# One product in two column parts near the start of long matmul runs: 64 and 192 columns in place of 256, in 44 places

## The chip, the core and the metric

The kernel runs on one core of a Trainium2 chip. TensorE (PE) multiplies, VectorE (DVE), ScalarE (ACT) and GpSimd (POOL) do the rest, and SyncE (SP) issues most of the transfers. The metric is the device time of one execution in microseconds (us).

## The reference

Two blocks act on x, 256 positions of 1024 features. The first is a layer with three attention branches and a feed-forward part with a short convolution; the second has two layers, each of a gated linear recurrence and a chunked matrix memory. Cut to the products that matter here:

```
x = x + rms_norm(merged(mla(h), dilated(h), memory(h)) @ w_o)      # h = rms_norm(x) ; w_in feeds the branches
x = x + rms_norm(gated_conv(rms_norm(x) @ w_ffn_up) @ w_ffn_down)
for l in range(2):                                                  # the second block
    rg_x, rg_z, ml_x, ml_o, ml_z = split((rms_norm(x) * (1 + scale) + shift) @ w_in_2[l])
    y = concat(rglru(conv(rg_x)) * silu(rg_z), mlstm(ml_x, ml_o) * silu(ml_z))
    x = x + gate * (y @ w_out_2[l])
```

All of it is float32.

## The kernel before

**Products.** Every weight matrix is read from HBM once, in blocks of 128 x 1024 numbers (`load`, lines 249 to 262). SP issues the transfer into a `raw` buffer, ACT rounds it to `hi` (line 257), DVE makes the rest `lo` = raw - hi (line 260). There are four buffers of each. The activations are split in the same way (H and L, or pairs of `s` tiles). A product in full precision is then three products of parts, hi·H, hi·L and lo·H, and `prod` (line 263 on) issues them for four blocks of 128 in the sum at a time: four matmuls of the first kind, four of the second, four of the third, so twelve. Each matmul has its own weights of 128 x 128, which are loaded just before it (the profile's PEld), and sends 256 columns through them (512 in a few places). All of them stand on line 269:

```
for b in range(0, len(terms), 4):
    for x, y in ((0, 2), (0, 3), (1, 2)):
        for t in terms[b:b + 4]:
            pe.matmul(dst, lhsT=t[x], rhs=t[y], start=(first and i == 0), stop=(last and i == n - 1))
            i += 1
```

**Callers.** `proj` makes 256 output features from two calls of `prod`, 24 matmuls each where the sum is over 1024 features: 48 in a row. `proj_long` has the activations as weights and the matrix as the moving side, two blocks of 128 positions, twelve matmuls a call. `proj_first` goes through `prod` too, one term at a time.

**Stages**, with the start in the profiled execution: the memory query `w_memq` (38 us) and then `w_c`; attention and gates (70); `w_o` (about 333); `w_up`, 22 projections of 48 matmuls, f = 0 by `proj_first` (358); `w_down` (503); then for each of two layers the input projections `w_mlx` and `w_rgx` (558 and 773), the small block products and gates, `w_rgz` (four projections, the last at 692 and 907), `w_mlz` (four, with two products of `of_head`, line 979, before each later one), and `w_out` (722 and 936).

**Order.** A scheduler places each engine's instructions from a model of how long each takes, and they then run in that order. Stretches under `urgent()` are placed early. Within a stretch on the TensorE the order is that of the code.

Of the kernel before, what the change touches and what calls it, by code (L numbers as in the profile page):

```python
# [19 lines left out]
S = 256  # L20
D = 1024
KT = D // P
# [4 lines left out]
URGENT = 1000  # L27
RAW, HI, LO = 4, 4, 4
FENCE = 4
STREAM, LOADED = 0, 16  # L30
FILL = dict(xn=8, cst=24, s=16, y=48, sx=16, pt=48, M=16, pts=56)
HOLD = 3
# [8 lines left out]
ADA_OUT = ((1, 3), (1, 3), (1,), ())  # L41
# [69 lines left out]
LONG = (256, 256, 256, 256)  # L111
# [87 lines left out]
def block_kernel(ctx: ExitStack, tc: tile.TileContext, T: dict, out: bass.AP):  # L199
    nc = tc.nc  # L200
    pe, act, dve, pool, dma = nc.tensor, nc.scalar, nc.vector, nc.gpsimd, nc.sync
# [59 lines left out]
        fence["n"] -= 1  # L261
        return hi, lo

    def prod(dst, terms, first=True, last=True):
        n, i = 3 * len(terms), 0
        for b in range(0, len(terms), 4):
            for x, y in ((0, 2), (0, 3), (1, 2)):
                for t in terms[b:b + 4]:
                    pe.matmul(dst, lhsT=t[x], rhs=t[y], start=(first and i == 0), stop=(last and i == n - 1))  # L269
                    i += 1  # L270

    def proj(name, j, kt, H, L, blks=None):
        nb = kt // 4
        if blks is None:
            blks = [load(T[name][j * nb + b]) for b in range(nb)]
        ps = mm_tile()
        for m in range(2):
            prod(ps[:, m], [
                (blks[k // 4][0][:, (k % 4) * 256 + m * P:][:, :P], blks[k // 4][1][:, (k % 4) * 256 + m * P:][:, :P], H(k), L(k))
                for k in range(kt)  # L280
            ])
        return ps

    def urgent(on=True):

        return tc.high_priority(offset=URGENT) if on else nullcontext()

    def proj_long(name, kt, j, H, L, hold=0, beside=(), pieces=LONG, at=16):

        w = pieces[j]  # L290
        ps = [mm_tile().rearrange("p a b -> p (a b)")[:, :w] for _ in range(2)]
        blks = _long_blocks(kt, pieces)[j]
        nb = len(blks)
        held = {}

        def part(b, t):
            tb = slice(t * P, (t + 1) * P)
            hi, lo = held[b]
            prod(ps[t], [(H(k)[:, tb], L(k)[:, tb], hi[:, i * w:(i + 1) * w], lo[:, i * w:(i + 1) * w])
                         for i, k in enumerate(blks[b][1])], b == 0, b == nb - 1)  # L300

        for b, (n, ks) in enumerate(blks):
            held[b] = load(T[name][n][:, :len(ks) * w], at)
            if b in beside:
                ada_steps(1)
            if b < nb - hold:
                for t in range(2):
                    part(b, t)
        for t in range(2):
            for b in range(nb - hold, nb):  # L310
                part(b, t)
        return ps
# [42 lines left out]
    H, L = kth(HT[0]), kth(HT[1])  # L355
# [171 lines left out]
    with tc.tile_pool(name="l1", bufs=1) as l1, tc.tile_pool(name="pS", bufs=1) as pS:  # L527
# [54 lines left out]


        for j in range(2):
            ps = proj("w_memq", j, KT, H, L)
            act.mul(mem_kq[:, 4 + 2 * j:6 + 2 * j], ps, HD_SCALE)


# [5 lines left out]
        for quarter in (0.0, 0.25):  # L594
# [10 lines left out]
            t = l1.tile([P, S], F32, name=f"trig{len(trig)}")  # L605
# [285 lines left out]
    def post_norm(name, kt, Hf, Lf, hold, g, sums, nxt, beside):  # L891
        z = rows_of(6)
        n = len(LONG) - 1
        acc = small.tile([P, 2, n + 1], F32, name="accn", tag="accn", bufs=2)
        for j in range(n + 1):
            jj = slice(LONG_AT[j], LONG_AT[j + 1])
            ps = proj_long(name, kt, j, Hf, Lf, hold, beside[j])
            if j == n:
                pre = [load(T[nxt][b]) for b in range(2)]
            else:  # L900
                for t in range(2):
                    sq = square_sum(ps[t], acc[:, t, j:j + 1])
                    dve.tensor_tensor(out=z[:, t, jj], in0=ps[t], in1=g[:, jj], op=ALU.mult)
            if j == 0:
                root_table(sq)
        x_sum = small.tile([P, 2, 2], F32, name="xsum", tag="xsum", bufs=2)
        stat = [Rstd(acc[:, t]) for t in range(2)]
        fl = Flip()
        for t in range(2):
            with urgent():  # L910
                square_sum(ps[t], acc[:, t, n:n + 1])
                ins = dve.tensor_tensor(out=z[:, t, jj], in0=ps[t], in1=g[:, jj], op=ALU.mult)
                rz = stat[t].get()
                for i, (a, b) in enumerate(PARTS):
                    dve.scalar_tensor_tensor(out=xn[:, t, a:b], in0=z[:, t, a:b], scalar=rz, in1=xn[:, t, a:b], op0=ALU.mult, op1=ALU.add)
                    if sums:
                        square_sum(xn[:, t, a:b], x_sum[:, t, i:i + 1])
                r = Rstd(x_sum[:, t]).get() if sums else None
            fl.add(t, r)
        return x_sum, fl, pre, ins  # L920
# [18 lines left out]
    aL = [slot(i, F32R, LOADED) for i in (3, 4, 5)]  # L939
    with tc.tile_pool(name="fp", bufs=2) as fp:  # L940
        for f in range(FT):
            ps = proj("w_up", f, KT, H, L) if f else proj_first(pre, H, L)
            u, z, w = (fp.tile([P, 2, S], F32, name=n, tag=n) for n in ("fu", "fz", "fw"))
            if f:
                with urgent():
                    dve.tensor_tensor(out=u, in0=ps, in1=rs.unsqueeze(1).to_broadcast([P, 2, S]), op=ALU.mult)  # L946
            else:
                for i in range(2):
                    dve.tensor_tensor(out=u[:, i], in0=ps[i], in1=rs, op=ALU.mult)
            for i in range(2):  # L950
                c = f + FT * i
                act.activation(z[:, i], u[:, i], AF.Identity, scale=col("conv_w", 88 + c), bias=col("conv_b", c))  # L952
                act.activation(w[:, i], u[:, i], AF.Identity, scale=col("conv_w", c))
                dve.scalar_tensor_tensor(out=z[:, i, 1:], in0=u[:, i, :S - 1], scalar=col("conv_w", 44 + c), in1=z[:, i, 1:], op0=ALU.mult, op1=ALU.add)  # L954
            pool.tensor_tensor(out=z[:, :, 2:], in0=z[:, :, 2:], in1=w[:, :, :S - 2], op=ALU.add)  # L955
            t = one()
            act.activation(t, z[:, 0], AF.Silu)
            dve.tensor_tensor(out=t, in0=t, in1=z[:, 1], op=ALU.mult)
            split(aH[f // 8][:, f % 8], aL[f // 8][:, f % 8], t)
# [59 lines left out]
    for l in range(2):  # L1019
# [42 lines left out]
        def mem_input(j):  # L1062
            jj = slice(2 * j, 2 * j + 2)
            if j:
                ps = proj(f"w_mlx{l}", j, KT, H, L)
                with urgent():
                    split(xmH[:, jj], xmL[:, jj], ps)
                ps = [ps[:, 0], ps[:, 1]]
            else:
                ps = proj_first(pre, H, L)  # L1070
                for m in range(2):
                    split(xmH[:, m], xmL[:, m], ps[m])
            cv = two()
            conv4(cv, ps, l, "ml_conv_w_2", "ml_conv_b_2", j)
            t = two()
            act.activation(t, cv, AF.Silu)
            split(xcH[:, jj], xcL[:, jj], t)
# [199 lines left out]
        sq = [numerator(0), numerator(1)]  # L1277
        for j in range(4):
            jj = slice(2 * j, 2 * j + 2)
            ps = proj(f"w_rgz{l}", j, KT, H, L)  # L1280
            silu_into(yrH[:, jj], yrL[:, jj], ps, hs[:, jj])
            if j < 2:
                norm_sums(j, sq[j])
                sq.append(numerator(j + 2))
            elif j == 2:
                norm_sums(2, sq[2])
                norm_sums(3, sq[3])
                with urgent():
                    dve.scalar_tensor_tensor(out=da, in0=ms[:, 0:S], scalar=1.0 / 256.0, in1=da, op0=ALU.mult, op1=ALU.add)
                    r0, w0 = one(), one()  # L1290
                    act.activation(r0, da, AF.Sqrt)
                    dve.reciprocal(r0, r0)
                    dve.tensor_tensor(out=w0, in0=r0, in1=r0, op=ALU.mult)
                    dve.scalar_tensor_tensor(out=w0, in0=w0, scalar=-0.5, in1=da, op0=ALU.mult, op1=ALU.mult)
                    dve.scalar_tensor_tensor(out=da, in0=w0, scalar=1.5, in1=r0, op0=ALU.add, op1=ALU.mult)
                    dp = in_parts("M", da)
            if l == 0:
                ada_steps(ADA_RGZ[j])
        ymH, ymL = slot(2, F32R, LOADED), slot(3, F32R, LOADED)
        for j in range(4):  # L1300
            jj = slice(2 * j, 2 * j + 2)
            ps = proj(f"w_mlz{l}", j, KT, H, L)
            pb = of_head(j, dp)
            for m in range(2):
                dve.scalar_tensor_tensor(out=hn[:, 2 * j + m], in0=hn[:, 2 * j + m], scalar=col("ml_norm_g_2", 8 * l + 2 * j + m),
# [10 lines left out]
        for j in range(n + 1):  # L1316
            jj = slice(LONG_AT[j], LONG_AT[j + 1])
            if j == n:
                ada_steps(50 - n_ada[0])
            ps = proj_long(f"w_out{l}", 2 * KT, j, lambda k: (yrH[:, k] if k < 8 else ymH[:, k - 8]),  # L1320
                           lambda k: (yrL[:, k] if k < 8 else ymL[:, k - 8]), 2 + l, () if l else ADA_OUT[j])
            if j == n:
                if l == 0:
                    pre = [load(T["w_mlx1"][b]) for b in range(2)]
# [43 lines left out]
```

## Time and profile before

| | us |
|---|---|
| median of 3 runs | 984.3 (982.62 to 986.07) |
| the profiled execution's own time | 990.15 |
| span of the profile, first to last instruction | 988.4 |
| PE busy in the span | 957.2 |
| PEld (weight loads) busy | 920.0 |
| DVE busy | 727.8 |
| ACT busy | 628.4 |

The profiled execution took 5.85 us more than the median of the runs that were timed. Busy times of PE are of pipelined instructions that overlap each other: a matmul's record is about 0.28 us long, and the next one starts after some 0.11 us. The distance from start to start, here called the pace, is what counts.

### The profile page before, as it was taken

Reading aid. Unit: us, or ns where it says so; the run is one execution under the profiler, and the core shown is the slowest. Engines: PE = TensorE matmul, PEld = TensorE weight load, DVE = VectorE, ACT = ScalarE, POOL = GpSimd, SP = SyncE. Lnnn points to the kernel's source line nnn. Section 1 sums busy time; section 2 is a strip of 40 time slices with the busy share of each in tenths; the row PEclk is TensorE's granted clock in tenths of the full one; section 3 lists DMA queues with packets and bytes.
Section 4 is the critical chain, followed back from the end, with each engine's and each line's share of the span. In section 5 each row is a group of like instructions: output and inputs, shape, how many; then the busy total and the mean of one; then the engine's idle time right before and its main releaser. Section 6 shows DMA issues by size and latency. Waiting matters only on the chain.

```text
span 988.4 us, 19653 instructions
## 1 busy us (share of the span) xinstructions
PE 957.2 (97%) x7880; PEld 920.0 (93%) x7880; DVE 727.8 (74%) x1283; ACT 628.4 (64%) x1042; POOL 53.1 (5%) x61
## 2 busy tenths in 40 slices
PE   7999999999999999999989999999999999999997
PEld 5999999899989989999989899898999988899997
DVE  5856776568475988878866798688976798687744
ACT  7666555453345578888753786895644776976552
POOL 0000000000000001121200000000001000000031
PEclk9999999999999999999999999999999999999999
DMA  8654566777776755555667365345786365235551
GB/s 298 210 183 141 176 231 194 242 242 227 245 259 192 254 187 189 193 189 179 204 221 244 123 219 174 124 140 190 254 254 215 124 191 170 97 119 193 188 175 63
DMA packets 53371, 190.74 MB, mean 193 GB/s; under 512 B 6080, under 2 KB 6464, under 8 KB 53280
## 3 DMA queue, kind: packets, MB, share of 16 engines
q1 hardware_dynamic: 52272, 185.17, 57.5%
q0 software_dynamic: 1008, 4.33, 1.4%
q8 instruction: 61, 1.00, 0.4%
q14 instruction: 30, 0.25, 0.1%
HBM read 188.42 MB, written 1.05 MB: 192 GB/s over the span
## 4 chain that ended last, share of the span: by engine, by line
PE 74%; DMA 9%; DVE 9%; ACT 4%; issue 3%; POOL 0%; DVEq 0%; SPq 0%; ACTq 0%; POOLq 0%
PE mm L269 64%; DMA raw<-in_w_ada 6%; DVE lo L260 4%; DMA raw<-in_w_down 1%; ACT hi L257 1%; PE sm L1059 1%; DVE raw L506 1%; DMA raw<-in_w_dv 1%; PE sm L1217 1%; DMA raw<-in_w_mlx 1%; PE sm L1268 1%; PE sm L269 1%; DVE two L1016 1%; PE sm L676 1%; PE sm L1259 0%
## 5 line engine op out<-in xcount | busy, mean ns | idle before, releaser
L260 DVE TENSOR_TENSOR lo<-raw,hi 128x1024 fp32r<-128x1024 f32 (+2 forms) x300 | 362.2, 1219 | 105.8 <-ACT hi L257 102.8
L257 ACT CAST hi<-raw 128x1024 fp32r<-128x1024 f32 (+2 forms) x300 | 308.6, 1039 | 159.8 <-PE mm L269 84.4
L269 PE MATMUL mm<-H,hi 128*128 128x256 f32 x1456 | 237.3, 281 | 0.1
L269 PE MATMUL mm<-H,lo 128*128 128x256 f32 x1456 | 233.6, 279 | 1.4 <-DVE lo L260 1.4
L269 PE MATMUL mm<-L,hi 128*128 128x256 f32 x1456 | 234.5, 279 | 0.4 <-DVE L L489 0.2
L269 PEld LDWEIGHTS mm<-H,hi 128*128 128x128 f32 x1456 | 198.3, 189 | 2.2 <-DVE s L1016 0.8
L269 PEld LDWEIGHTS mm<-H,lo 128*128 128x128 f32 x1456 | 197.3, 188 | 1.6 <-DVE lo L260 1.6
L269 PEld LDWEIGHTS mm<-L,hi 128*128 128x128 f32 x1456 | 197.6, 188 | 1.1 <-DVE L L489 0.6
L269 PE MATMUL mm<-hi,s 128*128 128x256 f32 (+1 forms) x1032 | 149.4, 285 | 0.2 <-ACT s L496 0.2
L269 PEld LDWEIGHTS mm<-hi,s 128*128 128x128 f32 x1032 | 132.6, 189 | 2.1 <-ACT s L496 0.4
L506 DVE CUSTOM_DVE_ANT_0 raw<-raw,c_act 128x1024 f32<-128x1024 f32 x48 | 59.3, 1236 | 64.9 <-DMA raw<-in_w_ada 64.7
L269 PE MATMUL mm<-lo,s 128*128 128x256 f32 (+1 forms) x516 | 85.5, 285 | 3.8 <-DVE lo L260 3.8
L269 PEld LDWEIGHTS mm<-lo,s 128*128 128x128 f32 x516 | 71.0, 189 | 5.3 <-DVE lo L260 4.4
L269 PE MATMUL mm<-s,hi 128*128 128x256 f32 x320 | 54.1, 288 | 0.0
L269 PEld LDWEIGHTS mm<-s,hi 128*128 128x128 f32 x320 | 44.7, 191 | 6.3 <-PE mm L269 2.5
L440 ACT ACTIVATE sq<-xn 128x256 f32<-128x256 f32 (+1 forms) x28 | 14.3, 509 | 45.3 <-POOL xn L1332 33.4
L269 PE MATMUL mm<-s,lo 128*128 128x256 f32 x160 | 34.4, 283 | 0.0
L952 ACT ACTIVATE fz<-fu,cols 128x256 f32<-128x256 f32 x44 | 26.2, 596 | 9.2 <-DVE fu L946 9.2
L955 POOL TENSOR_TENSOR fz<-fz,fw 128x508 f32<-128x508 f32 x22 | 24.8, 1127 | 110.0 <-DVE fz L954 110.0
L493 ACT CAST s<-two 128x512 fp32r<-128x512 f32 x24 | 14.9, 620 | 23.2 <-DVE two L1273 23.2
L659 ACT ACTIVATE sx<-sx,nm 128x256 f32<-128x256 f32 (+3 forms) x24 | 13.3, 556 | 23.7 <-DVE nm L656 23.7
L269 PEld LDWEIGHTS mm<-s,lo 128*128 128x128 f32 x160 | 25.5, 190 | 2.0 <-issue 1.2
(322 smaller groups left out, 1151.0 us busy)
## 6 DMA issues: line engine op xcount, KB each, us to landing
raw<-in_w_ada SPq DMA_DIRECT2D x48, 512.0 KB, 4.5
raw<-in_w_up SPq DMA_DIRECT2D x44, 512.0 KB, 4.3
raw<-in_w_out SPq DMA_DIRECT2D x32, 512.0 KB, 4.4
raw<-in_w_down SPq DMA_DIRECT2D x20, 512.0 KB, 4.3
raw<-in_w_mlx SPq DMA_DIRECT2D x16, 512.0 KB, 4.3
raw<-in_w_rgx SPq DMA_DIRECT2D x16, 512.0 KB, 4.4
raw<-in_w_mlo SPq DMA_DIRECT2D x16, 512.0 KB, 3.7
raw<-in_w_rgz SPq DMA_DIRECT2D x16, 512.0 KB, 4.1
```

Source lines behind the costliest of these rows:

```text
L257: act.copy(hi[:, :n], raw)
L260: dve.tensor_tensor(out=lo[:, :n], in0=raw, in1=hi[:, :n].bitcast(F32), op=ALU.subtract)
L269: pe.matmul(dst, lhsT=t[x], rhs=t[y], start=(first and i == 0), stop=(last and i == n - 1))
L440: return act.activation(sq[:, :src.shape[-1]], src, AF.Square, accum_out=acc)
L493: act.copy(hi, src)
L506: dve.tensor_tensor_reduce(out=raw, in0=raw, in1=c_act, op0=ALU.mult, op1=ALU.add, scale=1.0, scalar=0.0, accum_out=mod[:, l, m:m + 1])
L659: act.activation(sx[:, a:b], src, AF.Exp, bias=nm[:, i:i + 1], accum_out=den[:, i:i + 1])
L676: pe.transpose(ps[:, i * P:(i + 1) * P], sx[:, o:o + P], ident)
L952: act.activation(z[:, i], u[:, i], AF.Identity, scale=col("conv_w", 88 + c), bias=col("conv_b", c))
L955: pool.tensor_tensor(out=z[:, :, 2:], in0=z[:, :, 2:], in1=w[:, :, :S - 2], op=ALU.add)
L1016: dve.scalar_tensor_tensor(out=dst[:, m, s:], in0=ps[m][:, :S - s], scalar=col(wname, 32 * l + 8 * (3 - s) + c), in1=dst[:, m, s:], op0=AL ...
L1059: pe.matmul(gp[32 * g:32 * g + 32], lhsT=wif[:, l, idx], rhs=rhs, start=(i < 4), stop=(i >= 20))
```

## The change

`prod` takes a new argument, `parted`. Where it is true, the sixth matmul of the call (i == 5, the second of the hi·L kind) is made as two matmuls, of columns 0 to 63 and of columns 64 to 255, each with its own load of the same weights. What is computed is the same.

```diff
+PART = 64
...
-    def prod(dst, terms, first=True, last=True):
+    def prod(dst, terms, first=True, last=True, parted=False):
+
         n, i = 3 * len(terms), 0
         for b in range(0, len(terms), 4):
             for x, y in ((0, 2), (0, 3), (1, 2)):
                 for t in terms[b:b + 4]:
-                    pe.matmul(dst, lhsT=t[x], rhs=t[y], start=(first and i == 0), stop=(last and i == n - 1))
+                    for c in ((slice(0, PART), slice(PART, S)) if parted and i == 5 else (slice(None),)):
+                        pe.matmul(dst[:, c], lhsT=t[x], rhs=t[y][:, c], start=(first and i == 0), stop=(last and i == n - 1))
                     i += 1
...
-                         for i, k in enumerate(blks[b][1])], b == 0, b == nb - 1)
+                         for i, k in enumerate(blks[b][1])], b == 0, b == nb - 1, b in parted)
...
-            ps = proj("w_memq", j, KT, H, L)
+            ps = proj("w_memq", j, KT, H, L, parted=True)
...
-            ps = proj_long(name, kt, j, Hf, Lf, hold, beside[j])
+            ps = proj_long(name, kt, j, Hf, Lf, hold, beside[j], parted=(0, 1, 2) if j == 0 else ())
...
-            ps = proj("w_up", f, KT, H, L) if f else proj_first(pre, H, L)
+            ps = proj("w_up", f, KT, H, L, parted=f < 4) if f else proj_first(pre, H, L)
...
-                ps = proj(f"w_mlx{l}", j, KT, H, L)
+                ps = proj(f"w_mlx{l}", j, KT, H, L, parted=j == 1)
...
-            ps = proj(f"w_rgz{l}", j, KT, H, L)
+            ps = proj(f"w_rgz{l}", j, KT, H, L, parted=j == 3)
...
-            ps = proj(f"w_mlz{l}", j, KT, H, L)
+            ps = proj(f"w_mlz{l}", j, KT, H, L, parted=j == 0)
...
-                           lambda k: (yrL[:, k] if k < 8 else ymL[:, k - 8]), 2 + l, () if l else ADA_OUT[j])
+                           lambda k: (yrL[:, k] if k < 8 else ymL[:, k - 8]), 2 + l, () if l else ADA_OUT[j], parted=(0, 1, 2) if j == 0 else ())
```

Counted in the built program, 44 matmuls are parted: 4 in `w_memq`, 4 in `w_o`, 6 in `w_up` (f = 1 to 3), 6 in `w_down`, and in each layer 2 in `w_mlx`, 2 in the last `w_rgz`, 2 in the first `w_mlz` and 6 in `w_out`. PE has 44 matmuls more, and no other engine has more or fewer instructions than before; on the queues of SP and POOL the order is the same. Lines of the changed file are higher by 1 to 3 (269 becomes 272).

PE before, at the last `w_rgz` projection of the first layer; L1268 is the sum of squares ahead of it, the rows after it are line 269's products of H or L with `hi` or `lo`:

```order
L1268 MATMUL sm<-sq,ones_s 32x256 x4
L269 MATMUL mm<-H,hi 128x256 x4
L269 MATMUL mm<-L,hi 128x256 x4
L269 MATMUL mm<-H,lo 128x256 x4
L269 MATMUL mm<-H,hi 128x256 x4
L269 MATMUL mm<-L,hi 128x256 x4
```

PE after, at the same place:

```order
L1271 MATMUL sm<-sq,ones_s 32x256 x4
L272 MATMUL mm<-H,hi 128x256 x4
L272 MATMUL mm<-L,hi 128x256
L272 MATMUL mm<-L,hi 128x64
L272 MATMUL mm<-L,hi 128x192
L272 MATMUL mm<-L,hi 128x256 x2
L272 MATMUL mm<-H,lo 128x256 x4
L272 MATMUL mm<-H,hi 128x256 x4
L272 MATMUL mm<-L,hi 128x256 x4
```

The sixth matmul of the 24 became a pair; the second 24 of the projection have theirs at the same place.

DVE before, in `w_up`, from f = 1 on; `lo` is a load's second half, `fu` takes a finished projection out of its PSUM tile, `fz` and `one` are the convolution and the gate:

```order
L260 TENSOR_TENSOR lo<-raw,hi 128x1024
L946 TENSOR_TENSOR fu<-mm,rstd 128x512
L958 TENSOR_TENSOR one<-one,fz 128x256
L260 TENSOR_TENSOR lo<-raw,hi 128x1024
L494 TENSOR_TENSOR s_4250<-one,s_4247 128x256
L954 SCALAR_TENSOR_TENSOR fz<-fu,cols,fz 128x255 x2
```

DVE after, at the same place:

```order
L961 TENSOR_TENSOR one<-one,fz 128x256
L949 TENSOR_TENSOR fu<-mm,rstd 128x512
L261 TENSOR_TENSOR lo<-raw,hi 128x1024
L497 TENSOR_TENSOR s_4258<-one,s_4255 128x256
L261 TENSOR_TENSOR lo<-raw,hi 128x1024
L957 SCALAR_TENSOR_TENSOR fz<-fu,cols,fz 128x255 x2
```

The scheduler moved the gate of the projection before and the evacuation ahead of one `lo`, for three projections; some 50 such rows differ on DVE and 30 on ACT over the whole program, each by a few places.

## Rows read from the trace of the kernel before

**Rows 1.** The page, busy us (share of the span), instructions.

```profile
PE 957.2 (97%) x7880; PEld 920.0 (93%) x7880; DVE 727.8 (74%) x1283; ACT 628.4 (64%) x1042; POOL 53.1 (5%) x61
```

**Rows 2.** The page, shares of the chain that ended last.

```profile
PE 74%; DMA 9%; DVE 9%; ACT 4%; issue 3%; POOL 0%; DVEq 0%; SPq 0%; ACTq 0%; POOLq 0%
```

**Rows 3.** Windows: stretch, its us, then busy us (instructions) by engine, PEclk, DMA.

```profile
40.00:70.00 30.00, 30.00 (x267) 30.00 (x267) 20.64 (x33) 18.04 (x28) 0.00 (x0) 1.00 0.65 207
560.00:590.00 30.00, 30.00 (x267) 30.00 (x266) 28.57 (x46) 25.61 (x41) 0.00 (x0) 1.00 0.60 193
364.00:470.00 106.00, 106.00 (x903) 106.00 (x902) 84.93 (x132) 87.28 (x150) 19.62 (x18) 1.00 0.60 193
```

**Rows 4.** Chain of waits: start us, us, what; long runs of products.

```profile
31.52 38.95 PE mm L269 x315
335.55 18.67 PE mm L269 x162
363.08 107.90 PE mm L269 x916
471.00 1.06 ACT hi L257
503.64 3.94 DMA raw<-in_w_down
558.67 21.81 PE mm L269 x190
721.88 42.41 PE mm L269 x360
936.25 45.24 PE mm L269 x384
```

**Rows 5.** The same view: runs of 48 or 96 at the same place in both layers.

```profile
677.85 5.66 PE mm L269 x48
686.02 5.46 PE mm L269 x48
692.48 11.50 PE mm L269 x96
892.23 5.66 PE mm L269 x48
900.39 5.46 PE mm L269 x48
906.85 11.50 PE mm L269 x96
```

**Rows 6.** Timeline of PE: start us, us, instruction; products of 128 columns.

```profile
305.38 1.50 PE L803 MATMUL sm<-pt,s 128*128 128x128 f32 x12
306.72 1.15 PE L676 MATMUL sm<-cst,sx 128*128 128x128 f32 x9
```

**Rows 7.** Who waited on PE: us in total, times, longest.

```profile
PE mm L269 <- DVE lo L260: 6.6, 5, 1.8
PE sm L1059 <- ACT two L1095: 1.2, 2, 0.8
```

**Rows 8.** Chain of waits ahead of that second wait.

```profile
798.63 0.95 ACT hi L257
811.58 0.63 ACT two L1076
```

**Rows 9.** Windows of the first layer's last gates, columns as in rows 3.

```profile
692.40:698.10 5.70, 5.70 (x50) 5.70 (x49) 5.70 (x8) 3.69 (x6) 0.00 (x0) 1.00 0.76 248
```

**Rows 10.** Timeline of PE, start of a run that keeps the wider pace.

```profile
692.98 0.63 PE L269 MATMUL mm<-L,hi 128*128 128x256 f32 x4
693.45 0.63 PE L269 MATMUL mm<-H,lo 128*128 128x256 f32 x4
```

**Rows 11.** Timeline of PE, start of a run that takes the closer pace.

```profile
686.33 0.62 PE L269 MATMUL mm<-L,hi 128*128 128x256 f32 x4
686.78 0.62 PE L269 MATMUL mm<-H,lo 128*128 128x256 f32 x4
```

More of the change, by code (lines that the diff above doesn't have):

```diff
@@ L268, in prod, with proj @@
                 for t in terms[b:b + 4]:
-                    pe.matmul(dst, lhsT=t[x], rhs=t[y], start=(first and i == 0), stop=(last and i == n - 1))
+                    for c in ((slice(0, PART), slice(PART, S)) if parted and i == 5 else (slice(None),)):
+                        pe.matmul(dst[:, c], lhsT=t[x], rhs=t[y][:, c], start=(first and i == 0), stop=(last and i == n - 1))
                     i += 1
-    def proj(name, j, kt, H, L, blks=None):
+    def proj(name, j, kt, H, L, blks=None, parted=False):
         nb = kt // 4
@@ L280, in proj @@
                 for k in range(kt)
-            ])
+            ], parted=parted)
         return ps
@@ L286, in urgent, with proj_long @@
         return tc.high_priority(offset=URGENT) if on else nullcontext()
-    def proj_long(name, kt, j, H, L, hold=0, beside=(), pieces=LONG, at=16):
+    def proj_long(name, kt, j, H, L, hold=0, beside=(), pieces=LONG, at=16, parted=()):
         w = pieces[j]
```

## The prediction

> **What bounds the kernel.** I read the page first: PE is busy 97% of the span, its weight loads 93%, DVE 74% [rows 1], and 74% of the chain that ended last is PE [rows 2]. So time on PE is mostly time of the kernel, but a busy record does not say how fast the matmuls follow each other. For that I went to the windows. A window counts every record that touches it, so the pace is (window + 0.28 us, the length of one record) / count. In 40 to 70 and in 560 to 590 us that is 30.28 / 267 = 113.4 ns from matmul to matmul, in 364 to 470 us 106.28 / 903 = 117.7 ns [rows 3]. They are the same instructions: 128 x 128 weights, 256 columns. The granted clock is 1.00 in all three stretches, the 2.4 GHz level, so it is not the clock. PE and PEld are busy for the whole of each, so no other engine is waited for either.
>
> The chain of waits shows the same two paces run by run. A projection of 48 matmuls takes either 5.65 to 5.66 us or 5.44 to 5.47, and nothing between: 16 of the first kind, 15 of the second, of which some stand in the rows [rows 5]. Three things are to be seen there. First, a run keeps its pace: 916 matmuls of `w_up` take 107.90 us, 117.8 each, and the ends of both `w_out` stages 42.41 / 360 and 45.24 / 384, again 117.8 [rows 4]. Second, the pace is decided in the first few matmuls: in the run at 692 us two rows of four already start 0.47 us apart, in the run at 686 us 0.45 [rows 10, 11]. Third, the two layers, which execute the same code, agree at each place: 5.66 and 5.66, 5.46 and 5.46, 11.50 and 11.50 for 96 [rows 5]. So the pace belongs to what stands ahead of a run, and is not drawn by lot.
>
> The stretches that go at 117.8 and stand behind a place where the change parts a matmul are `w_up` and, in each layer, the run from the last `w_rgz` through `w_mlz` and `w_out`. `w_memq` and `w_mlx` are parted too and run at 113.4 already [rows 3], and `w_o`, with its start, at 18.67 / 162 = 115 [rows 4].
>
> **What the change adds.** 44 pairs of a weight load and a matmul. No row has a matmul of fewer than 128 columns behind a full weight load. The nearest is the run of 128-column products on line 803: the twelve start at 305.38 and what follows them at 306.72, 1.34 / 12 = 111.7 ns each [rows 6]. There, half the columns save 2 ns of 113.4, so the weight load and not the columns sets that pace. I take it for both parts: 2 x 111.7 in place of 113.4 makes 110 ns a place. Bounds: the parts go at the slow pace, 2 x 117.8 - 113.4 = 122; or they save what 111.7 saves against 117.8, 2 x 111.7 - 117.8 = 106. A price near or below nothing for the pair itself is excluded by PEld being busy 30.00 of 30.00 us [rows 3]: the second load has no room.
>
> Which of the 44 are on the path? In `w_down`, 6 are hidden: from 503.64 us the chain goes through transfers and loads, and PE waits 6.6 us for `lo` in five waits, most of them there [rows 4, 7]; without that cover they cost 0.66. Of `w_o`'s 4 two fall ahead of 335.55, where the chain still goes through DVE and ACT [rows 4]; price 0.22. The second layer's 2 in `w_mlx` are hidden, since at 798 to 812 us the chain is ACT's and PE then waits 1.2 us for `two` [rows 7, 8]; price 0.22. The other 34 (memory query 4, `w_o` 2, `w_up` 6, first layer 12, second 10) lie in runs that the chain takes whole: 34 x 0.110 = **+3.74 us**, bounds 3.6 and 4.15.
>
> The scheduler's moves on DVE and ACT put a gate and an evacuation ahead of one `lo`. In `w_up` that is hidden by the four buffers: DVE is busy 84.93 of 106 us there and PE never waits [rows 3]. If the cover were gone, a `lo` would be late by two operations, at 84.93 / 132 = 0.64 us on average, in three projections: 3.9 us at most. I take nothing.
>
> **What it may take away.** The slow pace, if a parted matmul ends it. The trace has no such place, so I argue from what the paces look like. A 64-column part is over long before the next weights are in; PE then stands still until they are, and so again after the 192. The next full matmul thus starts the moment its weights are there and the following load starts with it. Runs that begin behind 128-column products, where columns and load are about equally long, take either pace (686 and 678 us [rows 5]). I take it that a slack of more than half a load is a stronger push than those, that it leaves the quick pace, and that in a run already quick it changes nothing. This is the weak step. Both ends: all of the slow stretch turns, or none.
>
> If it turns, each slow matmul gives back 117.8 - 113.4 = 4.4 ns, of 117.8, or 3.7%. `w_up`: first parted at about 365.9, and it counts until 471.0, where the chain leaves PE [rows 4]: 105.1 us x 0.0374 = 3.93. After that the loads bind until `w_down` is half done, and a faster PE only waits longer. First layer: from 693.1 to the end of the products at 766.8, 73.8 us: 2.76. Second: 907.4 to 981.5, 74.1 us: 2.77. Together **-9.46 us**.
>
> **Sum.** 990.15 - 9.46 + 3.74 = 984.43 for the profiled execution, a factor of 0.9942. The timed runs had a median of 984.3, 5.85 lower; the same factor gives **978.6 us**. I scale because I can't tell whether the 5.85 lies in the paces or elsewhere.
>
> **A page against it.** The Trainium skill, "TensorE: Matmul & The Clock Gate", section "Back-to-back issue gap", gives a single matmul's gap as N / 2.4 + 2.5 ns. By it 64 and 192 columns together cost only 2.5 ns more than 256, and the 34 places 0.09 us. The same section says that in a stream of weight loads and matmuls both set the spacing, and line 803's 111.7 ns for 128 columns (the formula has 55.8) sides with that.
>
> **Rivals.**
> 1. *The parts cost, and the pace stays.* For: a pace outlives waits of a stage and the `of_head` products in between, 624 matmuls of the last run by the code. Then 990.15 + 3.74, on the timed scale 988.0. Worse by one mechanism: the push leaves the slow pace, and the quick runs fall into it as well, `w_memq` with `w_c` (31.8 us behind its first part), `w_o` (18.0) and the first `w_mlx` (27.2), 77.0 x 4.4 / 113.4 = 2.99 more: 991.0. It decides between gain and loss when less than 3.74 / 9.46 = 40% of the slow stretch turns.
> 2. *Only part turns, or was slow only in this execution.* `w_up` begins behind waits on other engines, so its pace may differ from run to run, and 3.93 is most of the 5.85 by which this execution was late. With the layers alone -5.53 + 3.74 = -1.79: 982.5.
> 3. *DVE becomes the bound.* From 692.4 to 711 us DVE is busy without a gap, 5.70 of 5.70 us at the head of it [rows 9]. If PE can't go faster there, 18.6 x 0.0374 = 0.70 comes back: 979.3. Against: a load's `lo` is ready one projection ahead, and the gain asked of it is 0.2 us per projection.
> 4. *The second weight load hides behind the part before it*, and the pair costs nothing: -9.46, 974.9. The page's formula amounts to this. Against: rows 3 and 6 as above.
>
> **Chances.** The forecast 0.50; rival 3 0.05, rival 4 0.03; rival 2 0.20; the pace stays 0.13, the quick runs turn slow 0.09. About 0.3% (2.95 us) is what a measurement of this kernel can tell from none. Forecast and rivals 3 and 4 are faster by more: 0.58. Rival 2 is within: 0.20. Both kinds of rival 1 are slower: 0.22. The range leaves out rival 4 and the worse kind of rival 1, and takes 988.0 with 0.5 for its price: 975.8 to 988.5. The forecast's own range is 977 to 981.
>
> **What would show it.** Right: parts of 64 columns followed after about 110 ns; `w_up`'s runs of 48 at 5.44 to 5.47 us and a window of 106 us there with some 937 matmuls; both `w_out` stages at 113.4. Wrong: 117.8 behind the parts; 5.66 where `w_mlx` and `w_c` had 5.45; new waits on `lo` at 692 to 722 us; or parts at well over 122 ns.

## The result, and the profile after

The changed kernel takes 994.75 us (median of 4 runs, 992.99 to 996.00), the kernel before 984.09 (4 runs beside it, 982.62 to 986.07): a ratio of 1.0106, 95% interval 1.0081 to 1.0131. It is 10.7 us slower, where 978.6 was forecast and 988.5 was the upper end. The profiled execution took 993.9 us, 3.8 more than the one of before that the prediction is built on.

The page of the kernel after, busy times and the shares of the chain that ended last, beside [rows 1, 2]:

```profile
PE 954.9 (96%) x7924; PEld 916.9 (92%) x7924; DVE 735.6 (74%) x1283; ACT 626.2 (63%) x1042; POOL 53.1 (5%) x61
PE 72%; DVE 10%; DMA 9%; ACT 5%; issue 4%; POOL 1%; DVEq 0%; ACTq 0%; SPq 0%
```

PE has 44 matmuls more and is busy 2.3 us less. What grew is idle time: who waited on PE over the whole span [rows 7], and the longest waits of 692 to 780 us, where the kernel before had none on `lo`:

```profile
PE mm L272 <- DVE lo L261: 11.0, 10, 3.8
...
PE mm L272 <- DVE lo L261: 3.3, 4, 1.5
PE sm L461 <- DVE diag L455: 2.0, 1, 2.0
```

The pace behind the parts is the one that was forecast. Windows of the kernel after, columns as in [rows 3]:

```profile
384.00:470.00 86.00, 86.00 (x761) 86.00 (x760) 74.54 (x107) 69.10 (x122) 16.30 (x15) 1.00 0.57 185
...
364.00:470.00 106.00, 106.00 (x935) 106.00 (x934) 89.93 (x129) 84.94 (x149) 19.56 (x18) 1.00 0.59 189
```

From 384 us on that is 86.28 / 761 = 113.4 ns, where [rows 3] had 117.7; 937 matmuls were forecast for the longer window. The chain of waits in the second layer, beside [rows 4, 5]: the first row is a projection ahead of the parts, the next is one behind them, and the last is `w_out` with its six pairs, 43.55 / 384 = 113.4 ns if a pair is taken at the 0.123 us below:

```profile
905.47 5.65 PE mm L272 x48
...
923.96 5.44 PE mm L272 x48
...
940.96 44.29 PE mm L272 x390
```

What a part costs, in the timeline of PE of the kernel after (a record of "x5" is four products, one of them parted):

```profile
41.52 0.73 PE L272 MATMUL mm<-L,hi 128*128 128x256 f32 x5
42.09 0.62 PE L272 MATMUL mm<-H,lo 128*128 128x256 f32 x4
...
43.01 0.62 PE L272 MATMUL mm<-L,hi 128*128 128x256 f32 x4
43.46 0.62 PE L272 MATMUL mm<-H,lo 128*128 128x256 f32 x4
...
44.37 0.73 PE L272 MATMUL mm<-L,hi 128*128 128x256 f32 x5
```

Four products with a pair take 0.57 us, four without 0.45; from pair to pair, 24 products, it is 2.85 us where 24 x 113.4 ns are 2.72. So a pair costs 0.12 to 0.13 us, against 0.110 forecast. By the formula for a single matmul in the Trainium skill, "TensorE: Matmul & The Clock Gate", section "Back-to-back issue gap", the estimate would be 2.5 ns; the rows do not agree.

The sign "parts of 64 columns followed after about 110 ns" did not come. Cut into narrower windows, the same timeline shows where the 64 columns, the 192 and the next full product start (the start is that of the first of two):

```profile
41.63 0.36 PE L272 MATMUL mm<-L,hi 128*128 128x64 f32 x2
...
41.66 0.48 PE L272 MATMUL mm<-L,hi 128*128 128x192 f32 x2
...
41.84 0.42 PE L272 MATMUL mm<-L,hi 128*128 128x256 f32 x2
```

In all 260 pairs of this study the 192 columns start 28 to 32 ns behind the 64, and the next product 169 to 175 ns behind the 192.

**Where the time goes.** PE executes the same matmuls in the same place in all kernels here (but for 12 places in `w_o`, where the tiles differ). With a pair counted as one, the k-th matmul of a trace can be set against the k-th of the profile of before, and the difference of their starts read along the program. The table, worked out from the records of PE, has all profiled executions of this study; its columns are places in the profile of before: ahead of `w_up` (353.6 us), end of `w_up` (481.9), in `w_down` (514.0), behind it (546.2), ahead of the last `w_rgz` of layer 1 (691.7), behind that layer's `w_out` (787.9), the last matmul (981.0).

```
us later than in the profile of before
                           353.6  481.9  514.0  546.2  691.7  787.9  981.0
before, second (e3)        +0.32  +0.32  +0.91  +0.72  +4.15  +4.16  +4.06
before, third (e12)        -0.52  -4.40  +0.21  -1.84  -0.10  -2.80  -4.96
after                      +1.33  -2.20  +6.57  +3.39  +2.49  +7.79  +3.77
44 parts, old order (e1)   +0.77  -2.12  +1.83  -0.36  -1.09  -1.88  -4.96
no parts, new order (e2)   -1.39  -5.37  +0.49  -0.89  -0.69  +5.55  +0.43
moves of w_down (e4)       -0.97  -4.06  +0.65  -2.53  -3.26  -4.17  -7.79
moves of layer 1 (e5)      +1.81  -1.51  +2.13  -0.31  -1.32  +5.15  +1.18
parts in w_up (e6)         -0.88  -3.99  +0.92  -0.78  -1.54  -1.53  -5.62
parts in layers (e7)       -0.01  -3.47  +2.47  +0.21  +2.10  +1.22  -1.94
10 parts (e8)              -0.20  -3.88  +0.96  -2.22  +0.01  -1.92  -6.09
layer 1 moves alone (e9)   -0.26  -4.37  +0.95  -1.09  -2.26  +1.40  +0.09
adaLN behind lo (e10)      +0.39  -2.96  +1.28  -0.76  -0.87  +1.90  -1.11
4 parts (e11)              -0.73  -0.74  -0.35  -2.58  -4.57  -6.71 -10.73
```

In the row of the kernel after, `w_up` gains 3.5 us, parts included. From there to the end of `w_down` 5.6 are lost, and 5.3 more from the last `w_rgz` to the second layer. The second of these losses is in no kernel that keeps the old order on DVE.

### The profile page after: what moved, and what is told of

It reads as the page before. It is cut to its first block, busy times and chain, and to the rows that moved or that the text cites. A ratio compares the mean times of both kernels' runs of the same rounds, so it can differ in the third digit from the quotient of the medians.

```text
span 992.2 us, 19743 instructions
## 1 busy us (share of the span) xinstructions
PE 954.9 (96%) x7924; PEld 916.9 (92%) x7924; DVE 735.6 (74%) x1283; ACT 626.2 (63%) x1042; POOL 53.1 (5%) x61
## 4 chain that ended last, share of the span: by engine, by line
PE 72%; DVE 10%; DMA 9%; ACT 5%; issue 4%; POOL 1%; DVEq 0%; ACTq 0%; SPq 0%
PE mm L272 61%; DMA raw<-in_w_ada 7%; DVE lo L261 4%; ACT hi L258 1%; PE sm L1062 1%; PE sm L272 1%; DVE raw L509 1%; DMA raw<-in_w_dv 1%; PE sm L679 1%; POOL xn L1335 1%; PE sm L1220 1%; PE sm L806 1%; ACT sq L443 0%; PE sm L461 0%; DVE s L1251 0%
## 5 line engine op out<-in xcount | busy, mean ns | idle before, releaser
L261 DVE TENSOR_TENSOR lo<-raw,hi 128x1024 fp32r<-128x1024 f32 (+2 forms) x300 | 369.0, 1242 | 98.2 <-ACT hi L258 94.6
L272 PE MATMUL mm<-H,hi 128*128 128x256 f32 x1456 | 234.8, 279 | 0.1
L272 PE MATMUL mm<-L,hi 128*128 128x256 f32 (+1 forms) x1478 | 234.5, 277 | 0.4 <-DVE L L492 0.2
L272 PE MATMUL mm<-H,lo 128*128 128x256 f32 x1456 | 231.2, 277 | 1.0 <-DVE lo L261 1.0
L272 PEld LDWEIGHTS mm<-H,hi 128*128 128x128 f32 x1456 | 195.9, 188 | 2.2 <-DVE s L1019 0.8
L272 PE MATMUL mm<-lo,s 128*128 128x256 f32 (+3 forms) x538 | 88.4, 286 | 8.9 <-DVE lo L261 8.9
L272 PEld LDWEIGHTS mm<-lo,s 128*128 128x128 f32 x538 | 73.2, 191 | 11.3 <-DVE lo L261 10.3
```

The costliest lines, as they stand in the source:

```text
L261: dve.tensor_tensor(out=lo[:, :n], in0=raw, in1=hi[:, :n].bitcast(F32), op=ALU.subtract)
L272: pe.matmul(dst[:, c], lhsT=t[x], rhs=t[y][:, c], start=(first and i == 0), stop=(last and i == n - 1))
```

## The experiments

In each comparison the kernel before was timed beside the others on the same chip; ratios are to it.

**The order, with and without the parts (e1, e2).** The built programs of both kernels say in which order DVE and ACT execute their instructions. An edge from each instruction to the one before it, with no wait added, holds a kernel to the order of the other; `own` is the engine's instructions as the code issues them. In such kernels the rows of DVE and ACT carry the line of the recording call (266 or 267), so they are read by their tiles, and PE's line 269 is 354 or 357.

```diff
+        for a, b in zip(order, order[1:]):
+            tc.add_manual_dep(own[b], own[a].name, mybir.DependencyInfo(mybir.DependencyClass.NoSync, mybir.DependencyReason.DATA), reason="pin")
...
+    dve.pin(tc, PINNED["DVE"])
+    act.pin(tc, PINNED["Activation"])
```

e1 is the changed kernel in the old order.

> The changed kernel with all 44 parted products, but the DVE and ACT instructions are held in the order that they have in the kernel before. Theory A (the parts speed the slow runs up as predicted, and what is lost is lost by the scheduler's new order on DVE and ACT): 977 to 981 us, no wait of PE on lo longer than about 2 us in 470 to 565 us and none in 692 to 768 us, the granted clock at 1.00 in 500 to 525 us. Theory B (the order is harmless; a faster PE runs into its loads, or the parts cost far more than 110 ns): like the changed kernel, 992 to 996 us, with the same waits. Theory C (the timed runs of the kernel before are not slow in w_up and the layers, so that there is nothing to gain, and the parts cost 3.7 us): 987 to 989 us.

Measured: 984.84 us, ratio 0.9986 (0.9967 to 1.0005). e2 is the kernel before in the new order (70 places on DVE, 29 on ACT).

> The kernel before, with no parted product, but the DVE and ACT instructions are held in the order that they have in the changed kernel. Theory A (the new order is what costs): 993 to 1000 us, with waits of PE on lo of 3 us and more near 500 us and several in 720 to 768 us. Theory B (order harmless): 984 us, within 1 us of the kernel before. Theory C (nothing to gain, parts cost 3.7 us, the rest is the order): 989 to 992 us.

Measured: 992.13 us, ratio 1.0064 (1.0041 to 1.0087). So the order costs without any part, and the parts without the new order cost nothing that can be told from no change. No theory has all of it. Theory A misses both times: e1 is not at 977 to 981 us and e2 is below 993, and near 500 us it is e1 that has a wait on `lo` of 3.6 us and a clock of 0.66, while e2 has no such wait above 1.8. B and C are out by e2 and e1. Between the changed kernel (1.0106) and e1 (0.9986) lie 1.2%, 11.8 us, which are the order's when the parts are there.

**Is the pace the place's? (e3, e12).** The kernel before, unchanged, twice more.

> The kernel before, unchanged, profiled in another execution. If the pace of a run belongs to its place in the program, the projections of w_up, the last w_rgz of each layer, and both w_out go at 117.8 ns a matmul again, and w_memq and w_mlx at 113.4. If it is drawn anew in each execution, some of these are quick here, and the 5.85 us by which the first profiled execution was late lie in them: w_up alone would be worth 4 us.

Measured: 994.22 us, 4.1 later than the first profile. `w_up` and both `w_out` at 117.8 again, but `w_mlx` of the first layer, quick in the first profile [rows 3], slow here. The windows:

```profile
364.00:470.00 106.00, 106.00 (x902) 106.00 (x902) 84.92 (x132) 87.43 (x151) 19.60 (x18) 1.00 0.60 192
560.00:590.00 30.00, 30.00 (x257) 30.00 (x256) 28.11 (x46) 25.43 (x40) 0.00 (x0) 1.00 0.58 186
700.00:760.00 60.00, 60.00 (x512) 60.00 (x511) 46.11 (x68) 32.10 (x45) 5.50 (x5) 1.00 0.74 238
...
910.00:960.00 50.00, 50.00 (x425) 49.41 (x422) 34.80 (x46) 28.51 (x38) 4.54 (x5) 1.00 0.54 177
```

The slow `w_mlx` is 1.3 us of the 4.1. Another 2.7 come between 672 and 681 us, and they are no pace: PE waits 2.97 us for `sq`, where the first profile had 1.76, and then goes on at a lower clock (the eighth field):

```profile
PE sm L1268 <- ACT sq L361: 3.0, 1, 3.0
...
677.00:682.00 5.00, 4.20 (x18) 2.92 (x19) 4.09 (x5) 4.85 (x6) 0.00 (x0) 0.66 0.40 116
```

> The kernel before, unchanged, profiled in a third execution. Its timed runs in the last comparison show a granted clock of 0.992 to 0.998, most of them 0.993 to 0.996, where the first profile (slow in w_up) has 0.998. Theory C (the timed runs are mostly quick in w_up, wait longer in w_down, and lose clock there): a clock of 0.992 to 0.996, w_up at 113.4 ns, a wait of over 3 us near 500 us, 980 to 987 us. Theory D (this program is slow in w_up in every execution): 117.8 ns there a third time, clock 0.996 to 0.998, 988 us and more.

Measured: 985.2 us, granted clock 0.994, as theory C has it. Its windows, the same stretches but for the second:

```profile
364.00:470.00 106.00, 106.00 (x938) 106.00 (x937) 92.45 (x134) 86.64 (x152) 20.11 (x19) 1.00 0.62 196
700.00:760.00 60.00, 60.00 (x532) 60.00 (x531) 46.61 (x70) 31.69 (x48) 7.14 (x6) 1.00 0.77 251
910.00:960.00 50.00, 50.00 (x427) 50.00 (x426) 31.68 (x41) 26.41 (x38) 7.71 (x8) 1.00 0.57 187
```

The same program, with no part in it, has `w_up` at 106.28 / 938 = 113.3 ns, the first layer quick, and the second slow (50.28 / 427 = 117.8). So the pace differs between executions of one program, and the first profile had the slow one in every stretch from which the change was to gain. The two profiles come from different chips, but that is not what decides it: e11 below, on the chip of e12, has no part ahead of the second block and went through the same products of `w_up` at 106.28 / 902 = 117.8 ns:

```profile
364.00:470.00 106.00, 106.00 (x902) 106.00 (x902) 84.94 (x133) 87.06 (x151) 19.57 (x18) 1.00 0.61 194
```

**Which moves cost (e4, e5, e9).** e4 and e5 are e1 with one group of the moves put back. In e5 it is the adaLN steps: each takes a block of `w_ada` in a raw buffer and sums it on DVE into `mod`, from which the scale, shift and gate of the second block come. The edit, at each of three projections of `w_mlz` (at the fourth place, the last `w_rgz`, it is the same step past other work):

```diff
+L506 raw,mod<-raw,c_act 128x1024
 L260 lo<-raw,hi 128x1024
 L1305 s<-s,cols,sm 128x256 x2
 L260 lo<-raw,hi 128x1024
 L1273 two<-two,s 128x512
-L506 raw,mod<-raw,c_act 128x1024
 L494 s<-two,s 128x512
```

> All 44 parted products, the old order on DVE and ACT but for the moves between the end of w_up and w_down (22 places on DVE, 2 on ACT), which stand as in the changed kernel. The old order with the parts gave 1.6 us less than the kernel before. Theory A (each group of moves makes its own loss where it stands): in the aligned traces the changed kernel loses 3.8 us more than the old order between 482 and 546 us, so this kernel comes out at 2.2 us above the kernel before, with a wait of PE on lo of 3 us and more near 500 us and the layers as in the old order. Rival (the loss needs the moves in w_up or in the layers): no change against the old order, 1.6 us below the kernel before.

Measured: 985.24 us, ratio 1.0007 (0.9986 to 1.0028), 0.2% above e1, to 0.28% either way: not to be told from it, and neither theory is decided.

> All 44 parted products, the old order but for the moves on DVE at the last w_rgz, w_mlz and w_out of the first layer (24 places: four adaLN steps ahead of the lo of two loads each), which stand as in the changed kernel. Theory A: the aligned traces differ by 6.1 us between 716 and 780 us, so this comes out at 4.5 us above the kernel before, with waits of PE on lo of 3 us in all at 715 to 770 us. Rival (these loads are covered, the loss there follows from what was late at 500 us): 1.6 us below the kernel before, as with the old order.

Measured: 992.07 us, ratio 1.0079 (1.0059 to 1.0100), so 0.93% or 9 us over e1 (to 0.28% either way), more than the 6.1 read from the traces. e9 has these 24 places alone, and no part.

> The kernel before with no part, old order but for the 24 places on DVE at the last w_rgz, w_mlz and w_out of the first layer, which stand as in the changed kernel. Theory A (the moves cost by themselves: an adaLN step waits for its transfer ahead of two lo, on an engine that had no gap there): 5 to 7 us above the kernel before, with DVE idle before the adaLN steps at 695 to 725 us. Rival (only a PE made faster by the parts is held up): within 1 us of the kernel before.

Measured: 990.28 us, ratio 1.0066 (1.0043 to 1.0090): 6.5 us, as theory A has it. That is as much as all the moves together cost in e2. So most of the loss is four adaLN steps that moved ahead of two `lo` each. What the changed kernel has above e5, 0.27%, is within the two intervals (0.32%).

**Why they cost (e10).** The timeline of DVE shows it. First e1, the adaLN step of each projection in the old order (`CUSTOM`), one after the other with no idle time:

```profile
702.37 1.22 DVE L267 CUSTOM_DVE_ANT_0 raw<-raw,c_act 128x1024 f32<-128x1024 f32 x1
...
707.78 1.22 DVE L267 CUSTOM_DVE_ANT_0 raw<-raw,c_act 128x1024 f32<-128x1024 f32 x1
...
713.18 1.23 DVE L267 CUSTOM_DVE_ANT_0 raw<-raw,c_act 128x1024 f32<-128x1024 f32 x1
```

Then the kernel after, in brackets the idle time ahead and what ended it:

```profile
701.49 1.23 DVE L509 CUSTOM_DVE_ANT_0 raw<-raw,c_act 128x1024 f32<-128x1024 f32 x1 [0.18 <-DMA raw<-in_w_ada]
...
707.29 0.69 DVE L497 TENSOR_TENSOR s<-two,s 128x512 fp32r<-128x512 f32 x1 [0.69 <-ACT s L496]
709.13 1.22 DVE L509 CUSTOM_DVE_ANT_0 raw<-raw,c_act 128x1024 f32<-128x1024 f32 x1 [1.14 <-DMA raw<-in_w_ada]
...
714.71 0.69 DVE L497 TENSOR_TENSOR s<-two,s 128x512 fp32r<-128x512 f32 x1 [0.69 <-ACT s L496]
716.21 1.23 DVE L509 CUSTOM_DVE_ANT_0 raw<-raw,c_act 128x1024 f32<-128x1024 f32 x1 [0.81 <-DMA raw<-in_w_ada]
```

Two things are to be seen. The adaLN step now comes before its transfer has landed, and two `lo` stand behind it. And `s` follows directly on `two`, so DVE stands still 0.69 us until ACT has rounded `two`; the adaLN step used to fill that gap. A projection took DVE 5.4 us (702.37 to 707.78) and now takes 7.64 and 7.08; PE needs some 5.7 for it, 48 products and the two of `of_head` (5.44 + 0.23). DVE was just quicker than PE and is now slower. The chain of the kernel after goes through these transfers, since in the code an adaLN step takes one of the four raw buffers of the loads, and these come free behind a `lo`:

```profile
696.73 4.73 DMA raw<-in_w_ada
...
704.22 4.88 DMA raw<-in_w_ada
...
711.52 4.67 DMA raw<-in_w_ada
```

e10 parts the two causes: the adaLN step stands behind the second `lo`, ahead of `two`.

> All 44 parts, old order but for the four adaLN steps at w_mlz of the first layer: each stands behind the second lo of its projection and just ahead of two (the gate's product), where the old order has it behind two and the changed kernel ahead of the first lo. In the changed kernel DVE is idle 2.65 us in four waits for the transfers of w_ada and 2.07 us in three waits for ACT's s behind two, the gap that the adaLN step used to fill. Theory A1 (the wait for the transfer is what costs): here the transfer has landed, and the time is that of the old order, 1.6 us below the kernel before. Theory A2 (the gap behind two costs as much): about 2 of the 4.7 us of idle time stay, some 2 to 4 us more than the old order, so up to 2.5 us above the kernel before.

Measured: 987.08 us, ratio 1.0031 (1.0012 to 1.0050), 3.0 us above the kernel before and 0.45% (4.4 us, to 2.7 either way) above e1: theory A2, a little beyond its sizes. In its timeline none of the four adaLN steps waits, and the gaps behind `two` are there (a further 0.26 us ahead of the first `lo`, for `hi`); a projection takes 6.53 us:

```profile
707.50 1.22 DVE L267 CUSTOM_DVE_ANT_0 raw<-raw,c_act 128x1024 f32<-128x1024 f32 x1
...
710.02 0.69 DVE L267 TENSOR_TENSOR s<-two,s 128x512 fp32r<-128x512 f32 x1 [0.69 <-ACT s L267]
...
714.03 1.22 DVE L267 CUSTOM_DVE_ANT_0 raw<-raw,c_act 128x1024 f32<-128x1024 f32 x1
```

So about half of the 9 us is the gap that the step no longer fills, and the rest, 0.48% from e10 to e5 (to 0.28% either way), goes with the wait for its transfer.

**What the parts are worth (e6, e7, e8, e11).** All in the old order, with fewer parts. e6 has those of `w_up` alone, e7 the 20 of `w_rgz`, `w_mlz` and `w_out`; e8 keeps ten, e11 four. From the edit of e8:

```diff
-            ps = proj("w_up", f, KT, H, L, parted=f < 4) if f else proj_first(pre, H, L)
+            ps = proj("w_up", f, KT, H, L, parted=f == 1) if f else proj_first(pre, H, L)
...
-            ps = proj(f"w_mlz{l}", j, KT, H, L, parted=j == 0)
+            ps = proj(f"w_mlz{l}", j, KT, H, L)
```

> Old order, and only the 6 parts in w_up. Theory C (the pace is drawn anew in each execution, and the timed runs of the kernel before are quick in w_up in most): the parts only cost, 6 x 0.12 = 0.7 us above the kernel before. Theory D (w_up is slow in the kernel before as in both of its profiles, the parts turn it, and w_down gives back about half): 3.9 - 0.7 - 1.9 = 1.3 us below it. In the trace all of w_up behind its first part at 113.4 ns by both; the layers, which have no parts here, go at 117.8 by D and at either pace by C.

Measured: 984.62 us, ratio 1.0000 (0.9982 to 1.0019). It lies between the two, and its interval holds both; the layers, with no parts, were slow in the first and quick in the second.

> Old order, and only the 20 parts in w_rgz, w_mlz and w_out of the two layers. Theory C (these stages are quick in most timed runs of the kernel before): the parts only cost, 20 x 0.12 = 2.4 us above it. Theory D (they are slow there as in both profiles): 5.5 - 2.4 = 3.1 us below it. In the trace w_up, which has no part here, goes at 117.8 ns by D and at either pace by C.

Measured: 985.48 us, ratio 1.0009 (0.9992 to 1.0027). The 3.1 us below of theory D are out. `w_up`, with no part here, was quick.

> Old order on DVE and ACT, and only 10 of the 44 parts: the two of w_up's f = 1, and in each layer the two of w_mlx and the two of the last w_rgz. Theory (a run keeps the quick pace once one or two parts have set it, and each further part only costs its 0.123 us of the PE path): 34 x 0.123 = 4.2 us less than with all 44 in the old order, which were 1.6 us below the kernel before, so 5.8 us below it; in the trace w_up and both w_out stages at 113.4 ns. Rival 1 (the pace has to be set again at each run, so that w_mlz and w_out fall back to 117.8): about the kernel before, within 1 us. Rival 2 (the other 34 parts lie beside other waits and cost nothing): 1.6 us below, as with all 44.

Measured: 983.38 us, ratio 0.9994 (0.9975 to 1.0013). 34 parts fewer are not the 4.2 us less of the theory. Rival 1 gives the right time for the wrong reason, since the pace held to the end of `w_out` in both layers. Rival 2, 1.6 us below, is within the interval too and is not excluded.

> Old order on DVE and ACT, and only 4 parts: the two of the last w_rgz in each layer. w_up is left as it is, since its gain came back in w_down in the runs so far. In the five executions so far that have no part there, about six of the ten stages from the last w_rgz to the end of w_out went at 117.8 ns. Theory (what is left to gain is the layers' slow share, 0.6 x 5.5 us, for 4 x 0.123 us): 2.8 us below the kernel before, 0.28%. Rival (the mixture of paces is worth nothing there either, as the 20 parts in the layers gave no gain): within 1 us of it. In the trace both stages at 113.4 ns by either.

Measured: 984.07 us, ratio 0.9981 (0.9958 to 1.0005): 1.9 us below, between the two and not told from either, nor from no change. No version here is faster by more than the measurement can tell.

The profile of e11 is the fastest of the study, 979.41 us, and it is slow in `w_up`. That points to where the gain of `w_up` goes. In the table each of the eleven executions with a quick `w_up` has lost 3.6 to 8.8 us between 481.9 and 514.0; e11 and e3, slow there, have lost 0.4 and 0.6. The windows show how. The kernel before, second execution (slow `w_up`), third execution (quick `w_up`), and the kernel after; the eighth field is the granted clock, 1.00 being 2.4 GHz:

```profile
500.00:505.00 5.00, 3.32 (x29) 3.12 (x27) 3.04 (x11) 3.85 (x6) 0.00 (x0) 1.00 0.23 92
505.00:510.00 5.00, 4.29 (x37) 4.29 (x38) 3.71 (x5) 1.21 (x2) 0.00 (x0) 1.00 0.70 232
```

```profile
500.00:505.00 5.00, 1.83 (x13) 1.83 (x14) 4.25 (x6) 0.94 (x2) 0.00 (x0) 0.92 0.35 115
505.00:510.00 5.00, 5.00 (x34) 5.00 (x34) 2.59 (x3) 1.67 (x2) 0.00 (x0) 0.74 0.84 277
```

```profile
505.00:510.00 5.00, 1.43 (x6) 1.43 (x7) 3.86 (x6) 0.37 (x1) 0.00 (x0) 0.78 0.31 100
510.00:515.00 5.00, 5.00 (x27) 5.00 (x26) 3.04 (x3) 1.67 (x2) 0.00 (x0) 0.54 0.79 267
```

A PE that comes to `w_down` 4 us earlier waits for the same `lo`, 3.5 us at the longest in e12 against 2.4 in e3, and then goes on at a lower clock. In the kernel after the wait is 3.83 us, and the clock's 0.54 costs 2.3 us in the 5 us behind it alone. An adaLN step's transfer stands ahead of that `lo` in its chain (4.41 us at 501.71), but e12 has one too (4.67 us at 496.06), so why the kernel after loses more there than the others (8.8 us against 3.6 to 5.9 by 514.0) is not shown. From 353.6 to 546.2 the eight executions with a quick `w_up` and the old order there have gained 1.0 us on average, parts included, of the 2.9 to 4.1 that they gained by 481.9; the two with a slow one differ from before's first profile by +0.4 and -1.9 over the same stretch.

## Why the prediction was wrong

The step that turned a gain into a loss is the term for the moves on DVE and ACT, put at nothing: they cost 6.3 us without the parts and 11.8 with them. And the 9.46 us on the other side of the sum were read from one execution, and the timed runs do not have them to give: e1, with the parts and without the moves, cannot be told from the kernel before.

**What bounds the kernel.** PE does, and the two paces are there within 0.1 ns in the windows above. The step that "the pace belongs to what stands ahead of a run, and is not drawn by lot" failed: e12 and e3 show one program with either pace in `w_up`, in the first `w_mlx` and in the first layer. What sets the pace of an execution is not known, and that both layers agreed place by place in the first profile does not recur: e12 has one quick and one slow. The three profiles of before took 985.2, 990.15 and 994.22 us, and its timed runs beside the experiments 978.6 to 991.8.

**What a part does.** It was named the weak step. The effect came, with weaker evidence than a count of places suggests, and the reason given for it was not borne out. Over all kernels here 22 parts stood behind products at 117.8 ns, and behind 20 of them it went at 113.4. But twelve of the 20 stand at the last `w_rgz`, and there the run was turning ahead of the part. From start to start, in ns, from the first product of that run on (worked out from the records of PE; a pair is in brackets):

```
first profile, layer 1 (no part)   222 117 118 118 117  118  118 118 117 119 117
e12, layer 1 (no part)             223 117 117 123 118  113  114 114 112 114 114
kernel after, layer 1              222 117 118 122 118 (200) 140 120 117 116 114
e1, layer 2                        222 117 118 118 117 (203) 142 115 123 118 114
```

A gap of 122 or 123 and one of 118 or 119 go ahead of the quick pace, with or without a part, and in the third row they stand ahead of the pair. Still, of the runs that began slow at this place all 13 with a part turned, and 2 of 9 without one. Of the ten other parts in slow stretches eight turned (one behind a gap of 1.39 us); the two that did not are in `w_up` of the kernel after, turned by the next part, and in `w_o` of e4. At the same 44 places in kernels that have no part there, 119 of 123 slow passages stayed slow. By stages, from the last `w_rgz` to the end of `w_out`: with parts all 16 were quick (e5's first layer but for a stretch behind a wait), without them 7 of 12 were slow from end to end. So a parted run does go over to the quick pace, and rival 1, both kinds, is out; of 230 parts in a quick stretch one was followed by a slow one. In `w_up`, however, the kernel after alone was slow ahead of its first part; the six others with parts there were quick already.

The mechanism was argued with a PE that stands still behind the 64 columns. By the starts it does not: the 192 follow after 0.03 us, and the time of the second load shows behind them. Why the turn can begin ahead of the part is open.

**What a part costs.** 0.123 us for 0.110; with 34 on the path 4.2 us for 3.74. That these 34 all count on the timed scale was not shown: e8 leaves out 34 too, 26 of them among these, 3.2 us by this price, and against e1 that gave nothing, within 2.6 us.

**What the change may take away.** For that one profile the sum comes out, 990.15 - 9.46 + 3.74 = 984.43, and e1, which has the parts and not the moves, was profiled at 985.17. That is luck in part, as the terms do not come out: by the table e1 gives back 1.8 us between 481.9 and 546.2, where the sum has nothing, and gains 0.8 from 691.7 to 787.9 and 3.1 behind that, where it has 1.7 each (2.76 or 2.77 less ten parts). Nor is it the gain over the timed runs, and the factor 0.9942 carried it there. The line "I can't tell whether the 5.85 lies in the paces or elsewhere" had the answer open, and the traces give part of it. e12 is 4.96 us ahead of the first profile: 1.3 from `w_up` through `w_down` and 2.7 in the first layer's stretch go with the quick pace, as rival 2 had it, but 1.7 come at 812 to 818 us, where the first profile has the wait for `two` [rows 7] and e12 has none, and e12 loses 1.6 behind such a wait in the first layer. e3, at nearly the same paces as the first profile, is 4.1 us later. So short waits set the executions apart as much as the paces do. Over e2, e7, e9, e11 and the three profiles of before, `w_up` without parts was quick in 4 of 7. And `w_up`'s 3.93 were counted up to 471 us although the loads bind behind it; most of it goes in the wait and the clock of `w_down`. With the old order the parts come out at 0.9986, nothing that can be told from no change, instead of 0.9942.

**The moves on DVE and ACT.** This is the step that made a loss of it: "I take nothing", with 3.9 us at most if the cover were gone. Only `w_up`'s moves were priced. Those of the first layer, four adaLN steps with their transfers, stood in the same comparison of orders and were given no price, though [rows 9] showed DVE without a gap there and rival 3 was built on that row. The rule that each move on an engine with no slack has to be priced by what is queued behind it would have found them. They cost 6.5 us alone (e9) and 9 with the parts (e5); all moves cost 6.3 without the parts (e2) and 11.8 with them, a difference just beyond what the intervals allow by chance. The rows of DVE give 4 projections x some 1.5 us, the smaller sizes. Why the moves should be dearer with the parts is not settled: that the parts make PE quick in every execution, where it is so in some without them, and so leave DVE less room, was only argued.

**A slip of the text.** It has `w_down` begin at 503 us. Counted by matmuls (21 projections of 48 behind f = 0), it begins at about 483; the wait at 503 lies within it. Its six parts so lie ahead of that wait, which changes no term, as they were taken as hidden by it.

**Open.** What sets the pace of a run that has no part, and how a part turns it. And whether the moves of `w_down` cost 0 or 4 us: e4 cannot tell. In its profile the loss of the kernel after is not there (1.5 us from 481.9 to 546.2, against 5.6), and the moves of `w_up` were in no run by themselves.

## What to carry to other kernels

Instructions added on one engine can change a scheduler's order on the others: compare the orders over the whole program, look first where the trace shows an engine without a gap, and ask of each move what now stands behind a wait and which gap it filled before. Then hold the order fixed and measure the edit by itself. And a stretch that differs between places in one profile may differ between executions of one program, so profile the kernel before at least twice before a difference in it is counted as something to gain.

## What was not expected of the hardware

A stream of weight loads and 256-column matmuls settles at 113.4 or 117.8 ns, with all operands ready and the clock at 1.00; one execution of a program takes the one and the next the other at the same place; and where the sixth product of a run was split into 64 and 192 columns, all 13 runs that began slow at the last `w_rgz` went over to the quick pace, against 2 of 9 without the split. The second part starts 0.03 us behind the first, and the next product 0.17 us behind that. Near 500 us a wait of PE of 3.2 us and more was followed in every profile by a granted clock of 0.54 to 0.79 over 5 us (the levels of 2.4 and 1.2 GHz mixed); waits of 1.8 (before, e11) and 2.4 us (e3) were followed by 1.00, but in e2 two waits of 1.84 and 0.71 us close together by 0.54, and in e3 one of 2.97 us at 677 us by 0.66. So a few microseconds gained ahead of a wait came back as clock.
